# Where the token selection is emitted, and how the normed input of four projections is made

## The chip, the cores and the metric

One core of one Trainium2 chip runs one launch of the kernel. The metric is the device time of one execution, in microseconds.

## What is computed

Three layers run one after the other on x, 512 tokens by 1024 features, in fp32: `third_block(second_block(first_block(x)))`.

```
rmsnorm(x, w) = x * rsqrt(mean(x*x) + eps) * w
swiglu(h)     = (silu(h @ w_gate) * (h @ w_up)) @ w_down        # hidden 2816

first_block:  h = rmsnorm(x); a Mamba2 scan and a gated delta net on h, merged, x += merged @ w_out
              x += swiglu(rmsnorm(x)); rmsnorm(x)
second_block: h = rms_norm(x, norm_w) * (1 + scale) + shift     # modulation from c @ w_ada
              p = h @ w_in  ->  r, k, v, w, a, g | q, k, v, gate, iq, ik, iw | merge gates
              ya = rwkv7_time_mix(...)                          # a chunked scan over the tokens
              yb = dsa_sparse_attention(q, k, v, iq, ik, iw)
              x += gate * ((sigmoid * ya + sigmoid * yb) @ w_o)
third_block:  x += 0.5 * swiglu(rms_norm(x)); gMLP and differential attention, merged
              x += 0.5 * swiglu(rms_norm(x))

dsa_sparse_attention, per block of 128 queries:
    sc        = einsum(iq, ik) * 64**-0.5
    idx_score = sum over 8 index heads of relu(sc) * iw;  -inf where the key's chunk is later
    sel       = top_k(idx_score, 128)
    softmax of q.k over the selected keys only, times v
```

## The kernel before, in words

**Linears.** Activations stand feature-major: eight tiles of 128 features by 512 tokens. Each fp32 product is made from three matmuls on split parts (`mm3`, L244 to L250: high weight by high input L248, high weight by low input L249, low weight by high input L250). A linear of 128 output columns (`lin_fm`, L252) is 24 matmuls of 128x512 for 1024 inputs, into one of two PSUM buffers (`pl`). Its weights come by one DMA of SP into `wr` (three buffers), ACT casts the high part into `wh` (L218, two buffers), DVE subtracts to get the low part `wl` (L219, two buffers). So each linear tile needs one `wl` subtraction from DVE before its first L250 matmul.

**Order.** The program is written as one stream of emitted instructions. The framework plans each engine's order when the kernel is built: whenever an engine is free in its plan, it takes the earliest emitted instruction that is ready. What is emitted later gives way to what is emitted earlier, and fills what that leaves. Tiles of one tag share a pool of buffers, and buffers are given out in the order in which the tiles are emitted. At run time every engine goes through its list in the planned order.

**Normed input.** `norm()` (L335) makes raw parts of x times gain (not yet divided by the root mean square; tags `tmpa`, `tmpb`), and then `rb`, the reciprocal root mean square spread over all partitions. `whole()` inside it makes the normed input itself: for each of eight feature tiles a DVE multiply (L390, into an `out` tile, four buffers), an ACT cast to the high part (L218, tag `h`) and a DVE subtraction for the low part (L219, tag `h`). A linear on raw parts can start before `rb` is there; its result is then multiplied by `rb` behind the matmuls.

**FFN.** `ffn()` (L542) is called three times (L1025 in the first block, L1717 and L1960 in the third). It has 22 hidden tiles, each a gate linear and an up linear, in three groups, then the down linears. The first two tiles use the raw parts, at the price of two more DVE operations each in `gate_epi` (L570, L574); at the third tile (`t == 2`) all eight pieces of the normed input are emitted at once. After each tile and each down epilogue one step of `aside` is emitted: in the first block's FFN alone this is the modulation of the second block, 26 steps, with its weights loaded through the `wr` buffers and its sums in `out` tiles (L1077, L1079).

**Second block.** It does the same by hand: three index-query linears (iq) run on raw parts with a multiply by `rb` behind them (L1139 to L1152), then a loop emits the eight pieces (L1155 to L1163: DVE multiply L1158, ACT cast with the shift L1160, DVE subtraction L1161), then come the fourth iq linear, the index keys, `wa_lin` and the rest. `score()` makes the index scores of query blocks 1 to 3 (256, 384 and 512 keys). `select()` (L1214) finds the 128th largest score of each row by 16 rounds of MAX8 (L1219) and MATCH_REPLACE8 (L1220) on DVE for each block and turns the scores into masks (L1221, L1222). Its eight maxima lie in a small tile `m8` (tag `small16`, twelve buffers). The RWKV part works in two halves of heads: `rkv_lin(b)` are six linears, `prep(b)` prepares, `scan(b)` is the chunked scan, whose triangular inverse (`tri_inv`, L490 to L511) is a chain of short DVE operations with two DMA round trips. `prep(1)` takes its small tiles from the same `small16` tag as `select()`, `prep(0)` and the scans from tags of their own. `g_lin` is four linears with the epilogue L1253, L1450; `q_lin`, `k_lin` and `v_lin` make the attention's inputs, with small tiles of the same tag in their epilogues (L204 and following). The masks are first read in `attend(b)` (L1549 on).

The order of emission is the one below; what stands earlier goes first wherever both are ready.

```python
    prep(0); scan(0); rkv_lin(1); select(); g_lin(); prep(1); scan(1); q_lin(); k_lin(); v_lin()
```

Of the kernel before, what the change touches and what calls it, by code (L numbers as in the profile page):

```python
# [11 lines left out]
F32 = mybir.dt.float32  # L12
# [4 lines left out]
AF = mybir.ActivationFunctionType  # L17
ALU = mybir.AluOpType
# [6 lines left out]
KB = D // P  # L25
# [8 lines left out]
class Env:  # L34
# [298 lines left out]
    def norm(self, x, gain, tm=None, between={}):  # L333

        nc = self.nc
        raw, acc = ([], []), None
        r = self.const([P, NC4], base="r")  # L340

        def root(sums):
            nc.vector.tensor_copy(r, self.rsqrt(sums, NC4, 1.0 / D, 1e-6))
            ps = self.spread(r)
            rb = self.tmp()
            nc.scalar.copy(rb, ps)
            return rb

        if tm is not None:
            ss = self.small(16)  # L350
        for k in range(KB):
            for tiles, stream in zip(raw, "ab"):
                with self.on(stream):
                    tiles.append(self.tmp(FR))
            hi, lo = raw[0][k], raw[1][k]
            col = gain[:, k:k + 1]
            if tm is None:
                src = x[k]
            else:
                with self.on(("a", "b", "")[k % 3]):  # L360
                    src = self.ps()
                for c in range(NC4):
                    nc.tensor.transpose(src[:, c * P:(c + 1) * P], tm[k // 4][c][:, (k % 4) * P:(k % 4 + 1) * P], self.ident)
            nc.scalar.activation(hi, src, AF.Copy, scale=col)
            nc.vector.scalar_tensor_tensor(lo, src, col, hi.bitcast(F32), ALU.mult, ALU.subtract)
            if tm is None:
                sq = self.tmp()
                nc.scalar.activation(sq, x[k], AF.Square)
                if k:
                    nc.vector.tensor_tensor(sq, sq, acc, ALU.add)  # L370
                acc = sq
                continue
            x.append(self.long())
            (nc.scalar.copy if k % 2 else nc.vector.tensor_copy)(x[k], src)
            between.get(k, lambda: None)()
            if k in (1, 5):
                for c in range(NC4):
                    at = k // 4 * 4 + c
                    nc.scalar.activation(self.tmp(), tm[k // 4][c], AF.Square, accum_out=ss[:, at:at + 1])
            if k == 5:  # L380
                nc.vector.tensor_tensor(ss[:, 0:4], ss[:, 0:4], ss[:, 4:8], ALU.add)
                rb = root(ss[:, 0:4])
        if tm is None:
            rb = root(self.token_sums(acc))

        def whole():
            hs, ls = [], []
            for k in range(KB):
                t = self.out()
                nc.vector.scalar_tensor_tensor(t, x[k], gain[:, k:k + 1], rb, ALU.mult, ALU.mult)  # L390
                h, l = self.hl()
                self.split(t, h, l)
                hs.append(h)
                ls.append(l)
            return hs, ls
        return raw, rb, r, whole
# [145 lines left out]
def ffn(env, x, gain, wg, g0, wu, u0, wd, hidden, scale, aside=iter(())):  # L542


    nc = env.nc
    raw, rb, _, whole = env.norm(x, gain)
    h = raw
    nt = hidden // P
    cuts = [nt * j // 3 for j in range(4)]

    def act_tile(j, n):
        if j != 1:
            return env.long(FR)
        with env.on("ab"[n % 2]):
            return env.tmp(FR)

    def wide(j):
        nonlocal h
        act = ([], [])
        for t in range(cuts[j], cuts[j + 1]):  # L560
            hold = []
            if t == 2:
                h = whole()
            early = t < 2
            def gate_epi(i, ps):
                t1 = env.tmp()
                g = ps
                if early:
                    g = env.tmp()
                    nc.vector.tensor_tensor(g, ps, rb, ALU.mult)  # L570
                nc.scalar.activation(t1, g, AF.Tanh, scale=0.5)
                nc.vector.scalar_tensor_tensor(t1, t1, 1.0, g, ALU.add, ALU.mult)
                if early:
                    nc.vector.tensor_tensor(t1, t1, rb, ALU.mult)  # L574
                hold.append(t1)
            def up_epi(i, ps):
                t1 = hold[0]
                nc.vector.tensor_tensor(t1, t1, ps, ALU.mult)  # L578
                hi, lo = act_tile(j, 0), act_tile(j, 1)
                env.split(t1, hi, lo)  # L580
                act[0].append(hi)
                act[1].append(lo)
            env.lin_fm(wg, g0 + t * P, P, h, gate_epi)
            env.lin_fm(wu, u0 + t * P, P, h, up_epi)
            next(aside, None)
        return act

    def down(j, act):
        def epi(i, ps):
            nc.vector.scalar_tensor_tensor(x[i], ps, scale, x[i], ALU.mult, ALU.add)  # L590
            next(aside, None)
        env.lin_fm(wd, 0, D, act, epi, k0=cuts[j], nk=cuts[j + 1] - cuts[j])

    first = wide(0)
    second = wide(1)
    down(0, first)
    third = wide(2)
    down(1, second)
    down(2, third)
# [496 lines left out]
def second_block(env, a, x, final=None):  # L1096
    nc = env.nc
# [6 lines left out]
    cols, gain, shift, gate = env.mod  # L1104


    both = gain
    if final is not None:
        both = env.const([P, 8], base="both")
        nc.vector.tensor_tensor(both, gain, final, ALU.mult)  # L1110
    raw, acc, accy = ([], []), None, None
    for k in range(KB):
# [3 lines left out]
        hi, lo = raw[0][k], raw[1][k]  # L1116
# [18 lines left out]
    rb = env.tmp()  # L1135
    nc.scalar.copy(rb, env.spread(r))

    iqt, early = [None] * 4, 3
    for i in range(early):  # L1139
        wh, wl = env.weights(w_in, 0, KB, IQ0 + i * P, P)  # L1140
        pb = env.ps()[:, 0:2]
        for k in range(KB):
            for n, part in enumerate((wh, wl)):
                mm(pb, part[:, k, :], env.shift2[:, 2 * k:2 * k + 2], start=k + n == 0, stop=k + n == KB)
        off = env.small(2)
        nc.vector.tensor_copy(off, pb)
        nc.vector.tensor_tensor(off[:, 0:1], off[:, 0:1], off[:, 1:2], ALU.add)
        ps = env.ps_lin()
        for k in range(KB):
            env.mm3(ps, wh[:, k, :], wl[:, k, :], raw[0][k], raw[1][k], k == 0, k == KB - 1)  # L1150
        iqt[i] = env.long()
        nc.vector.tensor_tensor(iqt[i], ps, rb, ALU.mult)  # L1152
        nc.scalar.activation(iqt[i], iqt[i], AF.Identity, bias=off[:, 0:1])

    h = ([], [])  # L1155
    for k in range(KB):
        t = env.out()
        nc.vector.scalar_tensor_tensor(t, x[k], both[:, k:k + 1], rb, ALU.mult, ALU.mult)  # L1158
        hi, lo = env.hl()
        nc.scalar.activation(hi, t, AF.Identity, bias=shift[:, k:k + 1])  # L1160
        nc.vector.scalar_tensor_tensor(lo, t, shift[:, k:k + 1], hi.bitcast(F32), ALU.add, ALU.subtract)  # L1161
        h[0].append(hi)
        h[1].append(lo)  # L1163
    def leave():
        if final is not None:
            ps = env.token_rstd(acc, 1.0 / D, 1e-6)
            for k in range(KB):
                nc.vector.scalar_tensor_tensor(x[k], x[k], final[:, k:k + 1], ps, ALU.mult, ALU.mult)
        return env.spill(x)
# [44 lines left out]
    def select():  # L1214
        for b in range(1, NC4):
            n, acc = (b + 1) * P, masks[b]
            m8 = env.small(8)
            for _ in range(16):
                nc.vector.max(out=m8, in_=acc[:, :n])  # L1219
                nc.vector.match_replace(out=acc[:, :n], in_to_replace=m8, in_values=acc[:, :n], imm_value=NEG)  # L1220
            nc.vector.tensor_scalar(acc[:, :n], acc[:, :n], -2.9e38, -1.0e30, op0=ALU.is_gt, op1=ALU.mult)  # L1221
            nc.vector.memset(acc[0:64, n - 64:n], -1.0e30)  # L1222
# [51 lines left out]
    def rkv_lin(b):  # L1274
        for i0 in (0, 4, 8):
            shift_lin(i0 + 2 * b, 2)
# [219 lines left out]
    def g_lin():  # L1496
        env.lin_fm(w_in, G0, 512, h, g_epi)
    def q_lin():
        env.lin_fm(w_in, Q0, 512, h, q_epi)
# [4 lines left out]
    def prep(b):  # L1504
        pre[b] = rwkv_half(b, (("a", "b"), ("", ""))[b])
    def scan(b):
        ys[b] = rwkv_scan(b, pre[b])
# [5 lines left out]
    prep(0)  # L1513
    scan(0)
    rkv_lin(1)
    select()
    g_lin()
    prep(1)
    scan(1)
    q_lin()  # L1520
    k_lin()
    v_lin()
# [76 lines left out]
    for f in range(4):  # L1599
# [4 lines left out]
        hi, lo = env.parts(gbt[f])  # L1604
# [4 lines left out]
    for k in range(8):  # L1609
        hi, lo = env.hl()  # L1610
# [3 lines left out]
    x = fetch()  # L1614
# [373 lines left out]
```

## Time and profile before

| | |
|---|---|
| median of three runs | 2966.54 us (2964.51 to 2968.52) |
| profiled execution | 2967.77 us, its span 2966.0 us |
| PE (TensorE matmul) busy | 2880.2 us, 97% |
| DVE (VectorE) busy | 1723.3 us, 58% |
| ACT (ScalarE) busy | 1107.8 us, 37% |
| mean granted TensorE clock | 0.987 of full speed |

The span is the stretch that the profile covers; what the execution's own time has beyond it is a constant. Busy time of PE counts overlapping matmuls once. PEclk is the share of full clock that was granted. In a timeline the bracket behind a row is the time for which the engine sat idle before it, and who ended that.

### The profile page before, as it was taken

Reading aid. Unit: us, or ns where it says so; the run is one execution under the profiler, and the core shown is the slowest. Engines: PE = TensorE matmul, PEld = TensorE weight load, DVE = VectorE, ACT = ScalarE, POOL = GpSimd, SP = SyncE. Lnnn points to the kernel's source line nnn. Section 1 sums busy time; section 2 is a strip of 40 time slices with the busy share of each in tenths; the row PEclk is TensorE's granted clock in tenths of the full one; section 3 lists DMA queues with packets and bytes.
Section 4 is the critical chain, followed back from the end, with each engine's and each line's share of the span. In section 5 each row is a group of like instructions: output and inputs, shape, how many; then the busy total and the mean of one; then the engine's idle time right before and its main releaser. Section 6 shows DMA issues by size and latency. Waiting matters only on the chain. (4 is left out here: it accounts for less than half of the span.)

```text
span 2966.0 us, 38950 instructions
## 1 busy us (share of the span) xinstructions
PE 2880.2 (97%) x14919; PEld 2380.8 (80%) x14919; DVE 1723.3 (58%) x3936; ACT 1107.8 (37%) x2086; POOL 47.5 (2%) x99
## 2 busy tenths in 40 slices
PE   7999999999999999989999999999999999999999
PEld 5878888888788886777878878888887978878887
DVE  7787737655655357987653563433667573554333
ACT  5435424433322234322353342222455562332221
POOL 1000000000000000000000000000000000000000
PEclk8999999999999999989999999999999999999999
DMA  5222233233445332222113423333322214333332
GB/s 139 69 71 67 73 93 93 66 102 93 140 140 169 91 96 87 77 57 52 46 33 89 124 81 100 94 99 100 125 72 71 65 58 128 100 93 96 97 93 92
DMA packets 481642, 269.03 MB, mean 91 GB/s; under 512 B 30591, under 2 KB 469056, under 8 KB 481456
## 3 DMA queue, kind: packets, MB, share of 16 engines
q1 hardware_dynamic: 445104, 254.62, 29.7%
q10 hardware_dynamic: 34512, 10.49, 1.4%
q0 software_dynamic: 1840, 1.43, 0.6%
q8 instruction: 118, 1.93, 0.3%
q14 instruction: 68, 0.56, 0.1%
HBM read 252.20 MB, written 14.16 MB: 90 GB/s over the span
## 5 line engine op out<-in xcount | busy, mean ns | idle before, releaser
L218 ACT CAST wh<-wr 128x1024 fp32r<-128x1024 f32 (+3 forms) x447 | 454.4, 1017 | 1288.4 <-PE pl L249 901.7
L250 PE MATMUL pl<-h,wl 128*128 128x512 f32 x2216 | 876.8, 396 | 13.9 <-DVE wl L219 13.8
L248 PE MATMUL pl<-h,wh 128*128 128x512 f32 x2216 | 878.4, 396 | 6.3 <-ACT wh L218 4.2
L249 PE MATMUL pl<-h,wh 128*128 128x512 f32 x2216 | 874.9, 395 | 0.0
L219 DVE TENSOR_TENSOR wl<-wr,wh 128x1024 fp32r<-128x1024 f32 (+3 forms) x447 | 526.2, 1177 | 439.8 <-ACT wh L218 433.9
L250 PEld LDWEIGHTS pl<-h,wl 128*128 128x128 f32 x2216 | 419.4, 189 | 103.7 <-DVE wl L219 17.4
L248 PEld LDWEIGHTS pl<-h,wh 128*128 128x128 f32 x2216 | 419.7, 189 | 97.2 <-ACT wh L218 6.5
L249 PEld LDWEIGHTS pl<-h,wh 128*128 128x128 f32 x2216 | 419.3, 189 | 86.3 <-issue 3.4
L250 PE MATMUL pl<-long,wl 128*128 128x512 f32 x648 | 253.3, 391 | 0.0
L249 PE MATMUL pl<-long,wh 128*128 128x512 f32 x648 | 252.9, 390 | 0.3 <-DVE long L219 0.3
L248 PE MATMUL pl<-long,wh 128*128 128x512 f32 x648 | 252.8, 391 | 0.0
L590 DVE SCALAR_TENSOR_TENSOR long<-pl,long 128x512 f32<-128x512 f32 x72 | 49.8, 691 | 175.9 <-PE pl L250 175.9
L249 PEld LDWEIGHTS pl<-long,wh 128*128 128x128 f32 x648 | 121.7, 188 | 25.7 <-DVE long L219 0.7
L250 PEld LDWEIGHTS pl<-long,wl 128*128 128x128 f32 x648 | 121.7, 188 | 25.4 <-issue 0.8
L248 PEld LDWEIGHTS pl<-long,wh 128*128 128x128 f32 x648 | 121.7, 188 | 24.8
L578 DVE TENSOR_TENSOR tmp<-tmp,pl 128x512 f32<-128x512 f32 x66 | 45.4, 687 | 150.0 <-PE pl L250 150.0
L248 PE MATMUL pl<-tmpa,wh 128*128 128x512 f32 (+1 forms) x312 | 125.0, 401 | 4.8 <-DVE tmp L685 2.8
L249 PE MATMUL pl<-tmpb,wh 128*128 128x512 f32 (+1 forms) x312 | 124.6, 400 | 0.0
L250 PE MATMUL pl<-tmpa,wl 128*128 128x512 f32 (+1 forms) x312 | 124.0, 397 | 0.0
L248 PEld LDWEIGHTS pl<-tmpa,wh 128*128 128x128 f32 (+1 forms) x312 | 59.4, 191 | 18.7 <-ACT h L218 3.5
L250 PEld LDWEIGHTS pl<-tmpa,wl 128*128 128x128 f32 (+1 forms) x312 | 59.3, 190 | 13.8 <-issue 0.5
L249 PEld LDWEIGHTS pl<-tmpb,wh 128*128 128x128 f32 (+1 forms) x312 | 59.3, 190 | 12.7 <-issue 0.3
(781 smaller groups left out, 3947.7 us busy)
## 6 DMA issues: line engine op xcount, KB each, us to landing
wr<-in_w_in SPq DMA_DIRECT2D x169, 512.0 KB, 3.9
wr<-in_w_ffn_in SPq DMA_DIRECT2D x44, 512.0 KB, 3.9
wr<-in_ffn_w_gate SPq DMA_DIRECT2D x44, 512.0 KB, 3.8
wr<-in_ffn_w_up SPq DMA_DIRECT2D x44, 512.0 KB
wr<-in_ffn_w_down SPq DMA_DIRECT2D x32, 448.0 KB, 3.6
wr<-in_w_ada SPq DMA_DIRECT2D x24, 512.0 KB, 3.6
wr<-in_w_out SPq DMA_DIRECT2D x16, 512.0 KB, 4.1
wr<-in_ffn_w_down SPq DMA_DIRECT2D x16, 512.0 KB, 3.9
```

The lines of the kernel that those rows point to most:

```text
L218: pin(self.nc.scalar.copy(hi, src))
L219: pin(self.nc.vector.tensor_tensor(lo, src, hi.bitcast(F32), ALU.subtract))
L248: mm(ps, wh, xh, start=first, stop=False)
L249: mm(ps, wh, xl, start=False, stop=False)
L250: mm(ps, wl, xh, start=False, stop=last)
L578: nc.vector.tensor_tensor(t1, t1, ps, ALU.mult)
L590: nc.vector.scalar_tensor_tensor(x[i], ps, scale, x[i], ALU.mult, ALU.add)
```

## The change

`whole()` now takes a number of pieces and goes on where it stopped. In an FFN the first three tiles use raw parts instead of two; one piece is emitted between a tile's gate and up linears and two behind its up linear, so that the eight pieces stand among the first three tiles. A step of `aside` is emitted only from the fourth tile on. In the second block the eight pieces stand behind the three raw iq linears, two, three and three. `select()` is emitted behind `scan(1)`, ahead of `q_lin()`.

```diff
-        def whole():
-            hs, ls = [], []
-            for k in range(KB):
+        hs, ls = [], []
+
+        def whole(n=KB):
+            for k in range(len(hs), min(KB, len(hs) + n)):
                 t = self.out()
                 nc.vector.scalar_tensor_tensor(t, x[k], gain[:, k:k + 1], rb, ALU.mult, ALU.mult)
...
-            if t == 2:
+            if t == 3:
                 h = whole()
-            early = t < 2
+            early = t < 3
...
             env.lin_fm(wg, g0 + t * P, P, h, gate_epi)
+            if early:
+                whole(1)
             env.lin_fm(wu, u0 + t * P, P, h, up_epi)
-            next(aside, None)
+            if early:
+                whole(2)
+            else:
+                next(aside, None)
...
+    h = ([], [])
+    def whole(k):
+        t = env.out()
+        nc.vector.scalar_tensor_tensor(t, x[k], both[:, k:k + 1], rb, ALU.mult, ALU.mult)
+        hi, lo = env.hl()
+        nc.scalar.activation(hi, t, AF.Identity, bias=shift[:, k:k + 1])
+        nc.vector.scalar_tensor_tensor(lo, t, shift[:, k:k + 1], hi.bitcast(F32), ALU.add, ALU.subtract)
+        h[0].append(hi)
+        h[1].append(lo)
...
         nc.scalar.activation(iqt[i], iqt[i], AF.Identity, bias=off[:, 0:1])
-
-    h = ([], [])
-    for k in range(KB):
-        t = env.out()
-        nc.vector.scalar_tensor_tensor(t, x[k], both[:, k:k + 1], rb, ALU.mult, ALU.mult)
-        hi, lo = env.hl()
-        nc.scalar.activation(hi, t, AF.Identity, bias=shift[:, k:k + 1])
-        nc.vector.scalar_tensor_tensor(lo, t, shift[:, k:k + 1], hi.bitcast(F32), ALU.add, ALU.subtract)
-        h[0].append(hi)
-        h[1].append(lo)
+        for k in ((0, 1), (2, 3, 4), (5, 6, 7))[i]:
+            whole(k)
...
     rkv_lin(1)
-    select()
     g_lin()
     prep(1)
     scan(1)
+    select()
     q_lin()
```

## Rows read from the trace of the kernel before

**Rows 1.** The page: busy time of each engine, share of the span, instructions.

```profile
PE 2880.2 (97%) x14919; PEld 2380.8 (80%) x14919; DVE 1723.3 (58%) x3936; ACT 1107.8 (37%) x2086; POOL 47.5 (2%) x99
```

**Rows 2.** A stretch: window, length, busy time of PE, PEld, DVE, ACT, POOL, clock, DMA.

```profile
1250.00:1300.00 50.00, 38.59 (x244) 32.55 (x243) 40.97 (x115) 11.46 (x22) 2.04 (x4) 0.83 0.19 46
```

**Rows 3.** Timeline of PE at the first linears on the normed input: start, duration, operation, [idle before].

```profile
755.43 0.39 PE L248 MATMUL pl<-h,wh 128*128 128x512 f32 x1
...
1129.12 0.39 PE L248 MATMUL pl<-h,wh 128*128 128x512 f32 x1
...
1133.73 0.79 PE L250 MATMUL pl<-h,wl 128*128 128x512 f32 x1 [2.92 <-DVE wl L219]
...
1145.29 0.39 PE L248 MATMUL pl<-h,wh 128*128 128x512 f32 x1
...
1774.03 0.39 PE L248 MATMUL pl<-h,wh 128*128 128x512 f32 x1
...
1779.40 0.80 PE L250 MATMUL pl<-h,wl 128*128 128x512 f32 x1 [3.14 <-DVE wl L219]
...
2616.51 0.39 PE L248 MATMUL pl<-tmpa,wh 128*128 128x512 f32 x1
...
2617.19 0.39 PE L248 MATMUL pl<-h,wh 128*128 128x512 f32 x1
```

**Rows 4.** Timeline of DVE at the same places.

```profile
782.07 0.69 DVE L578 TENSOR_TENSOR tmp<-tmp,pl 128x512 f32<-128x512 f32 x1 [1.39 <-PE pl L250]
...
1116.20 0.16 DVE L1146 COPY s<-pa 128x2 f32<-128x2 f32 x1 [1.30 <-PE pa L1144]
...
1132.46 1.22 DVE L219 TENSOR_TENSOR wl<-wr,wh 128x1024 fp32r<-128x1024 f32 x1
...
1769.99 0.75 DVE L390 SCALAR_TENSOR_TENSOR out<-long,cols,tmp 128x512 f32<-128x512 f32 x1
1770.65 0.69 DVE L572 SCALAR_TENSOR_TENSOR tmp<-tmp,tmp 128x512 f32<-128x512 f32 x1
...
1778.12 1.22 DVE L219 TENSOR_TENSOR wl<-wr,wh 128x1024 fp32r<-128x1024 f32 x1
...
1792.39 0.69 DVE L578 TENSOR_TENSOR tmp<-tmp,pl 128x512 f32<-128x512 f32 x1 [2.26 <-PE pl L250]
...
2630.19 0.69 DVE L578 TENSOR_TENSOR tmp<-tmp,pl 128x512 f32<-128x512 f32 x1 [2.26 <-PE pl L250]
```

**Rows 5.** Stretches of line L1219 and of line L1220: busy time of DVE.

```profile
1166.00:1291.00 125.00, 25.04 (x48) 0.92 0.25 65
...
1166.00:1291.00 125.00, 28.18 (x96) 0.92 0.25 65
```

**Rows 6.** Waits of PE in the stretch 1166 to 1291: total, times, longest.

```profile
PE pa L511 <- DMA tmpa<-blocks: 10.6, 1, 10.6
PE pa L1305 <- ACT long L1297: 2.7, 1, 2.7
```

**Rows 7.** Timeline of DVE in the same stretch: the weight subtractions around the triangular inverse.

```profile
1252.66 1.21 DVE L219 TENSOR_TENSOR wl<-wr,wh 128x1024 fp32r<-128x1024 f32 x1
...
1273.33 1.20 DVE L219 TENSOR_TENSOR wl<-wr,wh 128x1024 fp32r<-128x1024 f32 x1
```

**Rows 8.** A short stretch behind that wait, all engines.

```profile
1275.00:1280.00 5.00, 5.00 (x21) 4.58 (x21) 3.79 (x8) 0.38 (x2) 0.00 (x0) 0.50 0.76 195
```

**Rows 9.** Timeline of DVE: the last small tile of prep(1), the first of q_lin.

```profile
1373.33 0.17 DVE L1319 COPY s<-tmp 128x4 f32<-128x4 f32 x1
...
1375.63 0.17 DVE L204 TENSOR_SCALAR s<-pa 128x8 f32<-128x8 f32 x1
```

**Rows 10.** A stretch of scan(1), all engines.

```profile
1373.00:1427.00 54.00, 48.55 (x334) 41.79 (x333) 36.93 (x158) 15.07 (x28) 1.07 (x3) 0.94 0.24 61
```

**Rows 11.** The same stretch and the next, tile pl alone: busy time of PE.

```profile
1373.00:1427.00 54.00, 26.18 (x92) 0.94 0.24 61
...
1427.00:1460.00 33.00, 13.20 (x57) 1.00 0.23 60
```

## Prediction, on record before the changed kernel ran

> **What bounds it now.** The page first: PE is busy for 2880.2 of 2966.0 us, DVE for 58% and ACT for 37% [rows 1]. So the kernel is bound by matmuls, and a change that adds or removes none can only give back, or add, the 86 us in which PE is idle and the time that it spends at the lower clock. The second view is the table of stretches of 50 us, read for the ones in which PE falls short. The worst is 1250 to 1300, with PE at 38.59 of 50 and a granted clock of 0.83 [rows 2], and it lies where token selection, g_lin and the end of scan(0) run together. The third view is the timeline of PE at the four places where a linear first reads the normed input. There PE waits for a `wl` subtraction: 2.92 us at 1133.73 and 3.14 us at 1779.40 [rows 3]. These waits say that DVE had something else ahead of the weights; the timeline of DVE shows what [rows 4].
>
> The price of a place is measured against an undisturbed linear: from 2616.51 to 2617.19 three matmuls start, 0.2267 us each [rows 3], so 24 take 5.44 us, 48 take 10.88 us and 96 take 21.76 us.
>
> **Part A, pieces in the second block.** From the first matmul on the normed input (1129.12) to the first of `wa_lin` (1145.29) there are two linears, 16.17 us for 10.88 [rows 3]: 5.3 us are lost, 2.92 of them in one wait and the rest at a lower clock behind it. The subtraction that PE waits for starts at 1132.46, behind the pieces [rows 4]. The change adds no instruction; it emits the same 24 piece instructions earlier, among the raw linears. DVE has room there: it sat idle for 1.30 us before 1116.20, waiting for PE [rows 4]. The pieces are eight multiplies and eight subtractions of about 0.75 us; I take 0.66 us from start to start, as 1769.99 to 1770.65 shows for the like operation L390 [rows 4], which makes 10.6 us. In the trace they begin right behind 1116.20 and the late subtraction comes 16 us after that, 3 us past its use. They can't begin before `rb`, which the raw tiles' epilogues read too, so I let them begin about 2 us earlier and the subtraction come about 1 us late or just in time. I take -4.0 of the 5.3 (0 to -5.3).
>
> **Part B, pieces in the three FFNs.** The same reckoning from the first matmul on the normed input to the up epilogue L578, less 0.2 us in which the last matmul ends. First block: 755.43 to 782.07 holds four linears, 26.64 - 21.76 - 0.2 = 4.7 us lost. First FFN of the third block: 1774.03 to 1792.39, two linears, 18.36 - 10.88 - 0.2 = 7.3. Second: 2617.19 to 2630.19, 13.00 - 10.88 - 0.2 = 1.9 [rows 3, 4]. Together 13.9 us. In the worst one the late `wl` is at 1778.12, among pieces that were planned ahead of it [rows 4]. With a third raw tile the pieces are first read 10.88 us later, near 1785, while even in the trace they are nearly through when that `wl` starts; and a weight subtraction now has at most two pieces emitted directly ahead of it. What can still be late is one `wl` by one or two pieces, about 1 us for each FFN. What it adds is two DVE operations of 0.69 (L572's like) for the third tile of each FFN, six in all, 4.1 us; they are hidden while DVE is at 58%, and cost up to their 4.1 if it is the one waited for. What moves with it: in the first block the steps of `aside` begin at the fourth tile, so its 24 weight loads on SP's queue and their DVE sums come about one tile's worth of steps later. There are 43 calls left for 26 steps, and the modulation is first read in the second block, so nothing waits. The earlier pieces also no longer stand behind the sums' `out` tiles. I take three quarters, -10.5 (-13.9 to +4.1).
>
> **Part C, selection taken out of scan(0).** Selection is 48 MAX8 of 25.04 us and 96 rows of L1220 of 28.18 us between 1166 and 1291 [rows 5], and it stands above `g_lin` in the order. Where scan(0) waits for the triangular inverse, PE has only `g_lin` to fill with, and DVE subtracts one weight at 1252.66 and the next at 1273.33 [rows 7]: for 20.7 us the linears get no new low part. PE then waits 10.6 us for the DMA of the inverse [rows 6], and from 1271.3 to 1280 it runs at 0.50 of the clock [rows 8], so 8.7 us hold 4.3 us' worth of matmuls. A smaller place is a wait of 2.7 us [rows 6], with some 2 us of low clock behind it (estimate, by the ratio of the larger place). In all 10.6 + 4.3 + 2.7 + 2 = 19.6. Without selection there `g_lin`'s 21.8 us of matmuls can run in the 20.7 us hole. The inverse itself also gets shorter, since selection's operations stand among its own. I take -16 (0 to -19.6).
>
> **Part D, selection put behind scan(1).** When may it start? Its small tile `m8` shares a tag with `prep(1)`, whose tiles are now emitted first. The trace shows that tag being handed out in order: the last small tile of prep(1) is written at 1373.33 and q_lin's first epilogue follows at 1375.63 [rows 9]. So I expect selection to begin at about prep(1)'s end, 1373 in the times of before. From there it is above q_lin, k_lin and v_lin, and fills what scan(1) leaves of DVE: of 54 us DVE is busy 36.93 [rows 10], of which about 12 are weights and epilogues of the linears (estimate: four subtractions of 1.22 and about 7 of epilogues), so 29 us are left for it. The two shorter blocks have 256 and 384 of 1152 columns, by which they are 5/9 of the 53.2 us [rows 5], 29.6: they take just this stretch, and the linears get no `wl` meanwhile. PE ran 92 linear matmuls in it [rows 11]; I let 30 still run, one tile of 24 and a part on `wl` made before (estimate). The other 62 have to be made up later, where PE has no room, since it is busy for 97% of the span [rows 1]. 62 x 0.2267 = +14. If the third block's rounds starve the linears too, 57 more matmuls [rows 11] add 13, and a low clock behind the gaps about 3: +30. If selection fits without loss: 0. I take +14, which has rows for it. The masks are first read in `attend(1)`, emitted behind the three linears, of which q_lin and k_lin alone are 43.5 us of matmuls: a late mask has that to hide behind.
>
> A rule of the Trainium skill speaks against a clean sum here. "TensorE: Matmul & The Clock Gate" (Part 1) has the engine's clock throttled by default and released by activity, so a starved scan(1) would also run its own matmuls slower; the trace agrees for scan(0), where the clock is at 0.50 behind the 10.6 us wait [rows 6, 8]. By it D lies nearer its upper end.
>
> **The sum.** -4.0 - 10.5 - 16 + 14 = -16.5. The profiled execution took 2967.8 us (span 2966.0), 1.2 us over the median of 2966.5; so 2951.3 on its scale and **2950** on the runs' median.
>
> **Rivals.** (1) *Selection is not held back by the small tiles.* Then it starts at about 1166 as now, only with `g_lin`, prep(1) and scan(1) above it: C of -13 to -16 remains and D is near 0, sum -27.5 to -30: about 2938. For it: its inputs are ready at 1166. Against: the order of the tag [rows 9]. Chance 0.17.
>
> (2) *Slower: the linears starve through all of scan(1).* Selection's 53 us of DVE stand above q_lin, k_lin and v_lin until the third block is done, as `g_lin` found for 20.7 us [rows 7]; D is +34 (all 119 starved matmuls are 27, and 7 for the clock), A and B give 9 and C 16: +9, about 2976. It decides as soon as scan(1) loses more than the 30 us that the rest gives. For it: the third block alone starved `g_lin`. Against: DVE's chain in scan(1) leaves gaps, and linears can run ahead before 1373. Chance 0.13.
>
> (3) *The pieces do not move in effect.* The planner already places ready work early, and the waits come from two `wl` and two `pl` buffers. Then A and B give 3 and C and D cancel to -2: about 2961. For it: DVE's list already has pieces at 1769.99, ahead of the first use at 1774.03 [rows 3, 4]. Against: the `wl` at 1778.12 was planned behind pieces that no matmul needed yet. The Trainium skill, "Perfetto Trace Analysis" (Optimization Strategy), says that a gap repeating on the engine that should be saturated can mean that there is no buffer for the next tile; that would be this rival, and no row decides it. Chance 0.20.
>
> **How the numbers follow.** The forecast (2941 to 2958 with its own bounds) has 0.50, the rivals 0.17, 0.13 and 0.20. The range reaches from rival 1 with B at its full size, 2932, to a sum just above no change, 2968, where D is near +30 and the rest as forecast; most of rival 2 and the largest gains are left out, about 0.2. A measurement of this kernel can tell some 0.2% from no change, 5.9 us. Faster by more: all of rival 1, 0.46 of the forecast's 0.50 and half of rival 3: 0.73. Within: the other half of rival 3, 0.04 of the forecast and 0.03 of rival 2: 0.17. Slower: 0.10.
>
> **What would show it.** A: no wait for `wl` of 2 us before `wa_lin`, 16.2 us become 11 to 12. B: 26.6, 18.4 and 13.0 us, counted from the fourth tile on, lose under 1 us each. C: no 10.6 us wait for the inverse's DMA, and `g_lin` ends before scan(0) does. D: the first MAX8 lies behind prep(1)'s last small tile, and weight subtractions are missing for 25 to 30 us of scan(1), with a wait for `wl` at their end. If MAX8 begins near 1166 rival 1 holds; if the stretch from prep(1)'s end to q_lin's end grows by over 30 us rival 2 does. The forecast is wrong if the time is outside 2941 to 2958.

## The result, and the profile after

The changed kernel takes 3010.43 us in the median of four runs (3008.32 to 3020.42), the kernel before 2967.53 in the same session: a ratio of 1.0145 (95% interval 1.0131 to 1.0158), 43 us slower. The profiled execution is the slowest of the four, 3020.42 us with a span of 3018.6.

The page of the changed kernel, busy time and the row of the granted clock over 40 slices:

```profile
PE 2916.7 (97%) x14919; PEld 2420.0 (80%) x14919; DVE 1727.4 (57%) x3942; ACT 1107.3 (37%) x2086; POOL 47.4 (2%) x99
...
PEclk8999999999999999996699999999999999999999
```

The same instructions take PE 36 us longer, and the clock row has one low place, slices 19 and 20, some 1360 to 1510 us. All the rest is small beside it.

**The FFNs (B).** The timeline of DVE, up epilogues of the third and fourth tile of the third block's first FFN:

```profile
1846.31 0.69 DVE L579 TENSOR_TENSOR tmp<-tmp,pl 128x512 f32<-128x512 f32 x1 [1.98 <-PE pl L250]
...
1857.19 0.69 DVE L579 TENSOR_TENSOR tmp<-tmp,pl 128x512 f32<-128x512 f32 x1 [2.71 <-PE pl L250]
```

The fourth tile, now the first on the normed input, takes 10.88 us from epilogue to epilogue: 48 matmuls and no loss, where before two linears took 18.4 [rows 3, 4]. The other two FFNs take 10.88 us at this place as well.

**The second block's pieces (A).** Timelines of PE and of DVE, then a short stretch of all engines (columns as in [rows 2]):

```profile
1123.14 0.27 PE L1160 MATMUL pa<-shift,wl 128*128 128x2 f32 x1 [2.22 <-DVE wl L219]
...
1143.71 0.40 PE L248 MATMUL pl<-h,wh 128*128 128x512 f32 x1
```

```profile
1109.86 0.68 DVE L1168 TENSOR_TENSOR long<-pl,tmp 128x512 f32<-128x512 f32 x1
...
1121.20 0.75 DVE L1150 SCALAR_TENSOR_TENSOR h<-out,mod,h 128x512 fp32r<-128x512 f32 x1
1121.87 1.22 DVE L219 TENSOR_TENSOR wl<-wr,wh 128x1024 fp32r<-128x1024 f32 x1
```

```profile
1125.00:1130.00 5.00, 5.00 (x14) 4.04 (x14) 4.48 (x8) 2.11 (x3) 0.00 (x0) 0.50 0.27 82
```

The wait for `wl` is still there, one tile earlier: now the third raw linear's subtraction stands behind pieces. `wa_lin` starts at 1143.71, 1.6 us earlier than in [rows 3], but the first raw epilogue (L1168, at 1109.86) comes 4.3 us earlier than in the trace of before:

```profile
1114.21 0.68 DVE L1152 TENSOR_TENSOR long<-pl,tmp 128x512 f32<-128x512 f32 x1
```

So A lost 2.7 us in this trace.

**The hole of scan(0) (C)** is closed:

```profile
1250.00:1300.00 50.00, 48.24 (x355) 41.04 (x354) 31.22 (x92) 15.61 (x30) 4.08 (x8) 1.00 0.22 56
```

PE is busy for 48.24 us at full clock where it had 38.59 at 0.83 [rows 2]. That is 9.65 us of idle time and 38.59 x 0.17 = 6.6 us of clock: 16 us, the predicted term.

**Scan(1) (D)** is where the time went. Stretches of 20 us, all engines:

```profile
1380.00:1400.00 20.00, 2.08 (x9) 1.74 (x9) 20.00 (x78) 0.58 (x1) 0.00 (x0) 0.59 0.15 32
1400.00:1420.00 20.00, 19.58 (x93) 18.15 (x92) 10.64 (x31) 4.39 (x10) 0.00 (x0) 0.50 0.01 2
1420.00:1440.00 20.00, 19.70 (x133) 18.84 (x133) 12.29 (x42) 3.14 (x8) 2.62 (x5) 0.71 0.06 16
1440.00:1460.00 20.00, 6.84 (x60) 5.80 (x59) 19.52 (x84) 1.71 (x4) 1.51 (x3) 0.71 0.08 18
1460.00:1480.00 20.00, 15.14 (x68) 13.93 (x69) 15.27 (x49) 2.87 (x6) 0.00 (x0) 0.50 0.10 26
1480.00:1500.00 20.00, 17.90 (x85) 16.85 (x83) 8.24 (x52) 2.50 (x6) 0.00 (x0) 0.50 0.01 4
```

From 1380 to 1500 PE is idle for 38.8 us of 120. Its busy time, times the missing part of the clock, is another 34.9 us (row by row, as 19.58 x 0.50 = 9.8). Note that DVE is not full either: 10.64 of 20 and 8.24 of 20. The timeline of DVE and the summary of the line of MAX8 show where selection lies and what is missing:

```profile
1360.46 1.22 DVE L219 TENSOR_TENSOR wl<-wr,wh 128x1024 fp32r<-128x1024 f32 x1
...
1362.63 0.16 DVE L1328 COPY s<-tmp 128x4 f32<-128x4 f32 x1
1362.70 0.42 DVE L1228 MAX8 s<-long 128x8 f32<-128x256 f32 x1
...
1500.93 1.21 DVE L219 TENSOR_TENSOR wl<-wr,wh 128x1024 fp32r<-128x1024 f32 x1
```

```profile
L1228 DVE MAX8 s<-long x48: 397/541/686, 1362.7 to 1486.4; 128x8 f32<-128x256 f32 x16, 128x8 f32<-128x384 f32 x16, 128x8 f32<-128x512 f32 x16
```

Selection begins right behind prep(1)'s last small tile (1362.63), as predicted from the tag. It lasts 124 us, and its two shorter blocks, for which the prediction had 54 us, take 89 of them (to 1452.1). No weight is subtracted for 140 us. The waits of PE (1355 to 1500):

```profile
PE pa L512 <- DMA tmpa<-blocks: 19.6, 2, 17.6
PE pa L1478 <- DVE s L204: 10.5, 1, 10.5
```

Read the first PE row with care: the inverse's DMA is only what came last. PE had nothing else to do, because no linear was ready, and DVE was full from 1380 to 1400 with selection's rounds among the inverse's own operations. The second is a head norm of q_lin, whose small DVE operations are emitted behind selection.

### The profile page after: what moved, and what is told of

It reads as the page before. It is cut to its first block, busy times and chain, and to the rows that moved or that the text cites. A ratio compares the mean times of both kernels' runs of the same rounds, so it can differ in the third digit from the quotient of the medians.

```text
span 3018.6 us, 38969 instructions
## 1 busy us (share of the span) xinstructions
PE 2916.7 (97%) x14919; PEld 2420.0 (80%) x14919; DVE 1727.4 (57%) x3942; ACT 1107.3 (37%) x2086; POOL 47.4 (2%) x99
## 5 line engine op out<-in xcount | busy, mean ns | idle before, releaser
L248 PE MATMUL pl<-h,wh 128*128 128x512 f32 x2168 | 856.9, 395 | 2.4 <-ACT wh L218 2.2
L250 PE MATMUL pl<-h,wl 128*128 128x512 f32 x2168 | 855.3, 395 | 1.7 <-DVE wl L219 1.6
L249 PE MATMUL pl<-h,wh 128*128 128x512 f32 x2168 | 854.5, 394 | 0.0
L250 PEld LDWEIGHTS pl<-h,wl 128*128 128x128 f32 x2168 | 408.9, 189 | 87.7 <-issue 2.7
L248 PEld LDWEIGHTS pl<-h,wh 128*128 128x128 f32 x2168 | 409.2, 189 | 86.5 <-ACT wh L218 2.9
L249 PEld LDWEIGHTS pl<-h,wh 128*128 128x128 f32 x2168 | 408.8, 189 | 84.4 <-issue 3.7
L248 PE MATMUL pl<-tmpa,wh 128*128 128x512 f32 (+1 forms) x360 | 145.0, 403 | 5.3 <-DVE tmp L691 2.8
L250 PE MATMUL pl<-tmpa,wl 128*128 128x512 f32 (+1 forms) x360 | 144.5, 402 | 0.9 <-DVE wl L219 0.9
L249 PE MATMUL pl<-tmpb,wh 128*128 128x512 f32 (+1 forms) x360 | 144.7, 402 | 0.0
L248 PEld LDWEIGHTS pl<-tmpa,wh 128*128 128x128 f32 (+1 forms) x360 | 69.5, 193 | 21.6 <-ACT h L218 3.5
L250 PEld LDWEIGHTS pl<-tmpa,wl 128*128 128x128 f32 (+1 forms) x360 | 69.4, 193 | 16.9 <-DVE wl L219 1.4
L249 PEld LDWEIGHTS pl<-tmpb,wh 128*128 128x128 f32 (+1 forms) x360 | 69.5, 193 | 14.8
```

The costliest lines, as they stand in the source:

```text
L248: mm(ps, wh, xh, start=first, stop=False)
L249: mm(ps, wh, xl, start=False, stop=False)
L250: mm(ps, wl, xh, start=False, stop=last)
```

## The experiments

Ratios are against the kernel before, run beside each. The difference in us is the ratio less one, times 2967.5.

**One part at a time.** Each part alone on the kernel before.

```diff
# selection alone
     rkv_lin(1)
-    select()
     g_lin()
     prep(1)
     scan(1)
+    select()
```

> The kernel before with the selection behind scan(1) and nothing else. Theory S (selection starves the linears through all of scan(1): no weight subtraction stands in DVE's order between its first and last round): scan(0) gains about 15 us, the stretch behind prep(1) loses about 63, so +48, between 3010 and 3022 us. Theory P (the pieces of the normed input, which changed at the same time, crowd DVE and cost the time): C and D cancel as predicted, about -2, near 2965 us.

3020.25 us, 1.0173 (1.0160 to 1.0187): +51. Theory S's size, and not P's: moving selection costs all of the time and more.

The second block's edit alone (its diff stands ahead of the prediction):

> The kernel before with the second block's pieces among the raw iq linears and nothing else. From the trace of the changed kernel (wa_lin starts 1.6 us earlier where the stretch began 4.3 us earlier, and 2.4 us more go behind it): +2 to +5 us. The prediction's part A: -4 us. Theory P would need tens of us here.

2970.26 us, 1.0002 (0.9992 to 1.0011): nothing. The prediction's -4 lies outside the interval (-2.4 to +3.3 us), and +2 to +5 only touches it. A PE wait in 1100 to 1160 shows the trade, 2.2 us here for 2.92 before:

```profile
PE pa L1154 <- DVE wl L219: 2.2, 1, 2.2
```

The FFN edit alone:

> The kernel before with the FFN edit (three raw tiles, pieces among them, aside from the fourth tile) and nothing else. Part B as predicted and as the two traces differ at its ends: -10 us (-8 to -12), near 2957. Rival 3 (the pieces do not move in effect): -3 us.

2957.42 us, 0.9962 (0.9949 to 0.9974): -11, part B as predicted. The three parts add up to 51 + 1 - 11 = 41 of the 43 measured together. This version is faster than both kernels.

**Where selection runs.** First its small tile taken out of prep(1)'s order, on the changed kernel:

```diff
-            m8 = env.small(8)
+            m8 = env.sp.tile([P, 8], F32, name=env.name("m8"), tag="m8", bufs=3)
```

> The changed kernel with selection's small tile in a tag of its own, so that it no longer waits behind prep(1)'s small tiles; it is emitted at the same place. Theory S: MAX8 begins near 1166 again, its rounds fill what scan(0), g_lin and prep(1) leave of DVE, and the linears of scan(1) have their weights: about 60 us below the changed kernel, 2945 to 2955. If the place in the order of emission alone costs the time (selection above q_lin, k_lin, v_lin, whenever it runs): above 3000 still.

2958.34 us, 0.9961 (0.9949 to 0.9974), 3 us above Theory S's band. D is gone: one buffer's tag decided when selection starts (here MAX8 runs from 1164.9 to 1321.6). But the 16 us of C are gone too, since this equals the FFN edit alone. The stretches of this run show where:

```profile
1250.00:1300.00 50.00, 49.01 (x312) 41.05 (x311) 45.31 (x117) 20.38 (x36) 2.19 (x4) 1.00 0.22 56
1300.00:1350.00 50.00, 43.61 (x253) 34.52 (x253) 37.75 (x134) 11.95 (x23) 2.04 (x4) 0.80 0.18 46
```

The hole of scan(0) is closed and one in prep(1) is open. Two things changed there. `g_lin` ran earlier: of the linears' matmuls (tile pl, PE alone) this run has 112 in the first stretch and 47 in the second, the kernel before 57 and 88:

```profile
1250.00:1300.00 50.00, 28.06 (x112) 1.00 0.22 56
1300.00:1350.00 50.00, 17.01 (x47) 0.80 0.18 46
```

```profile
1250.00:1300.00 50.00, 16.77 (x57) 0.83 0.19 46
1300.00:1350.00 50.00, 24.31 (x88) 1.00 0.26 67
```

And the next filler, `q_lin`, stands below selection. The weight of its second tile was cast by ACT at 1289.28, and DVE subtracted it 36 us later, behind the last rounds:

```profile
1289.28 1.04 ACT L218 CAST wh<-wr 128x1024 fp32r<-128x1024 f32 x1 [1.93 <-PE pl L249]
```

```profile
1321.63 0.67 DVE L1228 MAX8 m<-long 128x8 f32<-128x512 f32 x1
...
1325.49 1.21 DVE L219 TENSOR_TENSOR wl<-wr,wh 128x1024 fp32r<-128x1024 f32 x1
```

Three more places were tried. Selection behind v_lin, in the shared tag:

```diff
     scan(1)
-    select()
     q_lin()
     k_lin()
     v_lin()
+    select()
```

> The changed kernel with the selection emitted behind v_lin instead of ahead of q_lin. Theory S (the loss is linears that stand below selection in the order): q_lin, k_lin and v_lin no longer starve, selection now starves only what is emitted behind it, the attention and the merge gates' linears, near the scan's end: 30 to 50 us below the changed kernel, 2960 to 2980. Rival B (the selection's 53 us of DVE cost the same wherever they are run late): above 3000.

2978.31 us, 1.0040 (1.0022 to 1.0058): inside Theory S's band. What stands behind selection now waits for it, `rwkv_out`'s epilogue (L1451) above all (a PE wait of the run, 1480 to 1560):

```profile
PE pa L1450 <- DVE long L1451: 19.5, 1, 19.5
```

Between k_lin and v_lin, in the shared tag:

> The changed kernel with the selection between k_lin and v_lin. Theory S: q_lin and k_lin, 43.5 us of matmuls, fill scan(1) ahead of selection, v_lin's 21.8 us and all behind it still give way: between the run with the selection last and the changed kernel, nearer the former, 2965 to 2985. Rival B: above 3000.

2981.34 us, 1.0042 (1.0027 to 1.0058): the same, and there v_lin's weights wait:

```profile
PE pa L279 <- DVE wl L219: 25.7, 1, 25.7
```

Behind v_lin with a tag of its own (the last two diffs together):

> The changed kernel with selection's small tile in a tag of its own and the selection emitted behind v_lin: it begins near 1166 and every linear up to v_lin goes first. Theory S: no linear starves, the hole that the run with the own tile alone showed in prep(1) (43.61 of 50 us at a clock of 0.80) closes: 2940 to 2950. Rival F (the hole comes from the scan's latency and only moves with the linears that could fill it): no better than that run, 2955 to 2960.

2968.24 us, 0.9996 (0.9988 to 1.0005): worse than the own tag alone, a miss for both. But prep(1) is full again, with `g_lin` used as early as in the run with the own tag alone; what differs is that `q_lin` now goes ahead of selection:

```profile
1300.00:1350.00 50.00, 48.60 (x324) 38.98 (x324) 43.79 (x149) 14.85 (x29) 2.57 (x5) 1.00 0.23 57
```

So selection held the filler of prep(1) back. The loss is now in scan(1), where DVE is full first and then has room:

```profile
1375.00:1400.00 25.00, 17.76 (x126) 14.12 (x124) 23.81 (x126) 4.12 (x7) 0.99 (x2) 0.86 0.21 47
1400.00:1425.00 25.00, 23.28 (x111) 22.17 (x110) 5.34 (x22) 5.67 (x12) 0.00 (x0) 0.50 0.14 44
```

Few linears run from 1390 on, though MAX8 ends at 1334 and weights were subtracted at 1396 and 1398. Why was not tried.

Part C without part D, on the kernel with the FFN edit, once behind `g_lin` and once in its middle:

```diff
     rkv_lin(1)
-    select()
     g_lin()
+    select()
     prep(1)
```

> The kernel before with the FFN edit and the selection between g_lin and prep(1), its small tile still ahead of prep(1)'s. The prediction's part C without part D: the hole at 1250 to 1280 closes and nothing else is lost, 16 us below the run with the FFN edit alone, 2940 to 2945. Rival F (the linears that fill one hole are missing in the next, here in prep(1), as in the run with the own tile): no better than the FFN edit alone, 2953 to 2960.

2963.36 us, 0.9987 (0.9972 to 1.0002): no better than the FFN edit alone, as Rival F had it, but 7 us behind it and just above that band. Prep(1) has 43.28 of 50 us at 0.86 in 1300 to 1350, and PE waits there for a subtraction (its waits, 1240 to 1350):

```profile
PE pl L250 <- DVE wl L219: 7.1, 2, 6.5
```

> The kernel before with the FFN edit and the selection between the second and the third tile of g_lin: two tiles, 10.9 us of matmuls, for the hole at 1250, two for prep(1). If filling is a matter of shares, both holes are halved, and their cost with the clock behind them more than that: 5 to 10 us below the FFN edit alone, 2947 to 2952. Rival F: 2953 to 2960.

2959.20 us, 0.9970 (0.9960 to 0.9981): F's number again, no gain from sharing.

Rival F held in number, but not in its reason. Where selection is out of prep(1) too, both holes stay closed. The run with selection alone (PE busy for 47.52 us of the first stretch, at 1.00), the linears (tile pl) first, then all engines:

```profile
1250.00:1300.00 50.00, 19.11 (x68) 1.00 0.21 56
1300.00:1350.00 50.00, 21.58 (x77) 1.00 0.23 56
```

```profile
1300.00:1350.00 50.00, 49.19 (x334) 41.10 (x332) 38.78 (x113) 19.92 (x38) 4.10 (x8) 1.00 0.23 56
```

There the hole takes only 11 linear matmuls more than before; most of it is filled by the scan's own, which come sooner without selection among its operations.

**What the loss in scan(1) is made of.** Fewer rounds first (`range(4)` for `range(16)`):

> The changed kernel with 4 of the 16 rounds of selection in each block, so the masks keep the 32 largest scores and not the 128: 13 us of DVE instead of 53, emitted at the same place. Theory S: the stretch without a weight subtraction shrinks with the rounds, from 127 us to some 35, and the loss in scan(1) from about 63 to about 15 us: 2955 to 2970. Rival O (the place in the order alone, through buffers handed out in order, holds the linears back): 2990 or above.

2961.44 us, 0.9974 (0.9964 to 0.9983): as Theory S had it, the loss goes with the length of selection. One head norm still waits for the short selection to end (MAX8 from 1359.2 to 1386.8):

```profile
PE pa L1478 <- DVE s L204: 17.5, 1, 17.5
```

Then the weights. `weights_parts` returns the high part twice for k_lin and v_lin:

```diff
+        if self.nolow:
+            hi = self.wp.tile(list(t.shape), FR, name=self.name("wh"), tag="wh", bufs=2)
+            pin(self.nc.scalar.copy(hi, t))
+            return [hi.rearrange("p (k f) -> p k f", k=nk)] * 2
```

> The changed kernel in which the weights of k_lin and v_lin get no low part: their matmuls are all there, but the third reads the high part again, so they need ACT's cast and no subtraction of DVE. Selection stands where it stands in the changed kernel. Theory S (the linears in scan(1) starve for DVE's subtraction alone): they fill scan(1), PE's clock stays up, and 45 to 60 us of the loss go: 2950 to 2970. Rival Q (selection's operations stand among scan(1)'s own chain on DVE and stretch it, whatever PE has to fill with; q_lin's small epilogues behind them hold PE up): 2985 or above.

3005.11 us, 1.0120 (1.0103 to 1.0136): only 7 us came back, so the subtraction is not the whole reason, and Theory S as it stood fell. Its linears (tile pl, PE) and the next epilogue on ACT show a second stop:

```profile
1375.00:1390.00 15.00, 14.61 (x64) 1.00 0.32 84
1390.00:1500.00 110.00, 0.20 (x1) 0.59 0.09 22
```

```profile
1379.35 0.60 ACT L1496 ACTIVATE long<-pl 128x512 f32<-128x512 f32 x1 [8.95 <-PE pl L256]
...
1506.23 0.59 ACT L1496 ACTIVATE long<-pl 128x512 f32<-128x512 f32 x1
```

The second k tile's epilogue writes a `long` tile at 1506; until then both PSUM buffers stay taken. So the head norms were left out as well (theory S2):

```diff
         nc.scalar.copy(qf[i], ps)
-        r = head_rstd(sq)
...
         nc.scalar.copy(kf[i], ps)
-        r = head_rstd(sq)
...
```

> The changed kernel in which the linears of k_lin and v_lin need nothing of DVE: no low part (their third matmul reads the high part again), and q_lin's and k_lin's epilogues leave out the head norm, so that they only copy on ACT; some 9 us of small matmuls go with it. In the run without the low part alone two k tiles ran and then nothing until selection was over, the epilogue of the next waiting for a buffer that q_lin's head norms, DVE work emitted behind selection, still held. Theory S2 (the linears stand still for two reasons, the weights and the buffers behind starved epilogues; with both gone they fill scan(1)): 2940 to 2962. Rival Q (selection's operations stretch scan(1)'s own chain, and that is what the time is): 2985 or above.

2935.88 us, 0.9886 (0.9871 to 0.9900). Selection still stands in scan(1), and PE is full (two of its stretches, PE alone, and MAX8's line):

```profile
1400.00:1420.00 20.00, 20.00 (x180) 1.00 0.15 41
1420.00:1440.00 20.00, 19.98 (x170) 1.00 0.12 30
```

```profile
L1234 DVE MAX8 s<-long x48: 405/547/696, 1352.4 to 1462.6; 128x8 f32<-128x256 f32 x16, 128x8 f32<-128x384 f32 x16, 128x8 f32<-128x512 f32 x16
```

From 1.0145 to 0.9886 are 77 us, of which some 9 are work left out. The other 68 are about the whole loss. Rival Q falls: the same rounds among scan(1)'s chain cost little once linears can run. The head norms alone left out:

> The changed kernel with q_lin's and k_lin's epilogues without the head norm (some 9 us of small matmuls less) and nothing else: the weights still need DVE's subtraction behind selection. Theory S2: either reason alone stops the linears, so little more than the work left out comes back, 2985 to 3003. If the buffers alone were the reason: 2940 to 2962, as the run without both.

2980.85 us, 1.0032 (1.0019 to 1.0046), 34 us below the changed kernel, 4 us below S2's band. The two reasons act together: without weights 7 us, without the epilogues 34 (about 25 besides the work left out), without both 77.

**The clock.** One 128x512 matmul ahead of each group of the second scan's inverse:

```diff
+        def heat(ps):
+            if warm is not None:
+                mm(ps, warm[:, 0:P], warm, start=True, stop=True)
```

> The changed kernel with one more 128x512 matmul on a normed-input tile ahead of each group of the triangular inverse's matmuls in the second scan, 32 in all, into the same PSUM tile, which the group then overwrites: 7.3 us of PE at full clock, work that nobody reads. Theory K (a good part of the loss is that scan(1)'s small matmuls run at the lower clock from the gap on, about 20 us by the stretches 1400 to 1425 and 1475 to 1500, and do not raise it themselves): the clock rises within the scan, the time falls by 10 to 25 us against the changed kernel, 2985 to 3000. If the small matmuls wait for DVE anyway, or the extra matmuls do not raise the clock: 3010 to 3020.

3000.95 us, 1.0111 (1.0094 to 1.0128): 10 us less with 7 us of work more. PE alone, stretches:

```profile
1385.00:1390.00 5.00, 5.00 (x22) 0.50 0.02 4
1390.00:1395.00 5.00, 4.83 (x35) 0.92 0.00 0
...
1400.00:1405.00 5.00, 4.83 (x43) 1.00 0.02 3
...
1425.00:1430.00 5.00, 0.35 (x2) 0.50 0.14 29
...
1440.00:1450.00 10.00, 9.94 (x38) 0.50 0.00 1
```

Theory K holds in part: the clock rose at 1391 and stayed up to the next gap. It did not rise between 1438 and 1455, where eight extra matmuls came with one chunk's groups alone. So some 10 us of the loss at least go with the clock; the edit also changed the planned order inside the scan a little, which was not kept apart.

## Why the prediction was wrong

**B** and **C** were right where they were measured: -11 for -10.5, and a hole closed of 16 us for 16. In C the size agrees better than the reason: `g_lin` was to fill the hole, and it was mostly the scan's own matmuls, coming sooner (68 linear matmuls for 57 in the run with selection alone).

**A** failed at "the subtraction come about 1 us late or just in time". I counted DVE's work up to the fourth linear and not who stands behind the pieces on the way: the third raw linear's own `wl` did, for 2.2 us, with the clock at 0.50 behind it. Measured 0 for -4.

**D** failed: +14 for about +67 (selection alone costs 51 with C's -16 in it). The place and the start were right: selection began behind prep(1)'s last small tile and the linears stood below it. The term that was mis-sized is how long they starve. I took scan(1) at its old pace, 54 us, let 30 of the 92 linear matmuls still run and let the third block's rounds leave room; the linears starved for 140 us. Three things drew it out. No weight at all was subtracted meanwhile, as g_lin's 20.7 us without one [rows 7] had shown on a small scale; rival 2 was that mechanism, with +34 for D. Then the head norms, DVE work behind selection too, held buffers, so that linears with their weights would have stopped as well (the runs without the one, the other and both: 7, 34 and 77 us). And with no linears to run, PE fell to half clock, so scan(1) and with it selection's own rounds went slower; DVE was idle for almost half of 1400 to 1420. I had nothing for the clock in the +14, 3 us in its upper bound and 7 in rival 2; the rows of after have 35.

"TensorE: Matmul & The Clock Gate" (Part 1) in the Trainium skill, weighed in the prediction, pointed the right way: a starved scan does run its own matmuls slower. The rows agree, 0.50 from 1400 to 1420. That activity releases the throttle did not come out there: PE was busy for 19.58 of these 20 us and stayed at 1.2 GHz.

**The sum** lost nothing by C in the changed kernel: with selection out of scan(0) and prep(1), both are full. But C holds only there. Three versions without D's loss were no faster than the FFN edit alone. In two of them the rounds still ran above `q_lin` around prep(1), and a weight of it that ACT had cast waited 36 and 35 us for its subtraction: D's mechanism on a small scale. In the third, with `g_lin` in two halves, both holes stayed half open. With q_lin, k_lin and v_lin ahead of selection and a tag of its own, prep(1) was full, and the run lost in scan(1) instead, for a reason that stays open. The run without weights and head norms fits C as a gain, -34 for -11 of B, -9 of work left out and some -14, but no run has C alone with no other loss.

**Rival 1** was answered by the run with the own tag: it is what happens without the shared tag, but at 2958, not 2938, since selection then holds `q_lin` back in prep(1). **Rival 3** was wrong for the FFNs. For the second block its size was right and its reason was not: the pieces did move, and another subtraction came to stand behind them.

## What to carry to other kernels

Before long work of one engine is moved in a planned order, list everything emitted behind the new place that needs this engine, epilogues that hold buffers included: it all waits until the long work ends, and an average of 58% busy says nothing against that. Ask then what the bounding engine runs meanwhile; if the answer is "only a latency chain", take the chain at the pace that the trace shows for it alone at the lower clock. And before counting a filled hole as a gain, ask what fills it and what the next stretch fills itself with: in prep(1) the next filler stood behind the work that had been moved.

## What the runs showed of the hardware

A PE that the profile calls busy can stay at the lower clock for long. In the run with the selection last, all engines, PE's busy time first:

```profile
1390.00:1430.00 40.00, 40.00 (x188) 38.24 (x187) 9.54 (x36) 9.08 (x20) 2.10 (x4) 0.50 0.05 14
1430.00:1435.00 5.00, 5.00 (x48) 3.94 (x46) 4.72 (x27) 0.03 (x1) 0.00 (x0) 0.98 0.18 54
```

For 40 us PE was busy without a gap, mostly with the scan's 128x64 and 128x128 matmuls (170 of 188; eight were 128x512), and was granted 0.50, 1.2 GHz; it came back to 2.4 GHz at 1430, when 64x128 matmuls and four of 128x512 ran among them. The shapes alone do not decide it. In the run with the selection between k_lin and v_lin the same stage, with no 128x512 matmul in these 12 us, ran at the full clock that it came in with:

```profile
1403.00:1415.00 12.00, 12.00 (x114) 11.53 (x112) 3.09 (x8) 4.71 (x11) 1.52 (x3) 1.00 0.01 1
```

In the run with extra 128x512 matmuls the clock rose at 1391, where two chunks' groups ran side by side, and did not between 1438 and 1455, where one chunk's ran alone.
